# A decoder trunk with transposing DMAs: the transposes of a pass four blocks later in SP's order

## The chip, the cores and the metric

The kernel runs on one core of a Trainium2 chip. The metric is the device time in microseconds of one execution; several runs are taken and their median is used.

## The reference

Two decoder layers over one sequence of 256 tokens, width 2048, all in float32. The first mixes by pooling, the second by causal attention in blocks; both also attend to 256 memory tokens. Cut to what matters:

```python
for i in range(2):
    if i == 1:
        k_blocks, v_blocks, k_mean = moba_shared_kv(h, w_kv_shared)
    u = h @ w_in[i]                                   # (256, 2048) @ (2048, 4096)
    branch_in, gate_b, mem_q, gate_m = jnp.split(u, [1536, 3072, 3584], axis=-1)
    branch = multiscale_pool(branch_in, ...) if i == 0 else moba_attention(branch_in, ...)
    mem_o = memory_attention(mem_q, mem, w_mem_kv[i])  # 4 heads of 128
    mixed = concat([branch * silu(gate_b), mem_o * silu(gate_m)])
    h = layer_norm(4 ** 0.25 * h + mixed @ w_out[i], ln_g[i], ln_b[i])
```

`multiscale_pool` takes trailing means over 2, 4, 8 and 16 tokens in four groups of 384 columns, subtracts the token, and applies a 384 x 384 matrix per group and a scale. With 256 tokens and blocks of 256 the second layer's attention is plain causal softmax attention with 12 heads.

## The kernel before

**Blocks.** All weights are read once, in blocks of 128 x 1024 floats (512 KB; the pool matrices in pieces of 768 and 384 columns). The whole program is one list, `items`, of such blocks. `run()` walks over it; at step i it issues, in this order:

- `prep(i + 3)`: ACT writes the block's high part `wh`, VectorE the rest `wl = raw - wh` (`split`, L71 and L72). There are four `raw` buffers and four `wh`/`wl` pairs.
- `load(i + 4)`: the load into a `raw` buffer, on SP's queue (L99, L101). It waits until VectorE has split block i, which had that buffer.
- `consume` of block i: matmuls on TensorE, twelve with 512 columns for a whole block (high x high, high x low, low x high), into PSUM `acc`.
- the functions that were filed for step i with `later(n, fn)`, which means "n steps from now".

Each engine executes its instructions in the order in which they were issued, so this list is also the order on SP, ACT, VectorE and TensorE. An activation is split in the same way and stays in `xm` (the two halves `xT` and `memT`) or `zT`.

**Turned passes.** A pass (`proj_n`, eight blocks) gives 512 columns of a product with the tokens on the partitions, in two tiles t = 0, 1 of 128 tokens. Keys, queries, pool inputs and gates are needed with the columns on the partitions, and `turned` does that: ACT takes a float's two 16-bit halves apart ("planes", `pl`, L273), two transposing DMAs on SP's queue (L274) turn the planes of one t each, and later VectorE joins the halves (`join`, two copies, L284). There are 20 such passes, 8 of them for gates, in which ACT first forms a tanh (L268) and VectorE a product (L269) ahead of the planes. For keys and queries (`heads`) ACT then writes the high part (L291) in the step of the join and VectorE the low part (L292) one step later.

**Attention.** `plan(pr, a, turns, b, c)` files a pair of heads: at step `a` after the query pass the scores (matmuls into `s` from `kk` and `qq`), then exponentials (L330), division, 32 x 32 transposes on VectorE (`turns`, L354), splits of the probabilities `pp` (`b`), and the products with the values and the gating (`c`). The second layer does this in three groups of four heads: a group is a pass of keys (`w_sk`), of queries and of gates (`w_in`) and of values (`w_sv`, not turned; its split weights land in `memT`).

**Pool layer.** Three times a pass of four column tiles, then their gates; the small pool matrices are woven between the blocks of the following pass, and the gate tiles lie in a ring of seven slots.

Of the kernel before, what the change touches and what calls it, by code (L numbers as in the profile page):

```python
# [13 lines left out]
U16 = mybir.dt.uint16  # L14
AF = mybir.ActivationFunctionType
ALU = mybir.AluOpType
AX = mybir.AxisListType

P = 128
# [18 lines left out]
SLOTS = 7  # L38
# [2 lines left out]
LD0 = 8  # L41
IDLE = 9
LP = 3
JOIN = 3


@with_exitstack
def trunk(ctx: ExitStack, tc: tile.TileContext, a: dict, out: bass.AP):
    nc = tc.nc
    ctx.enter_context(tc.manual_schedule())  # L50
    sb = ctx.enter_context(tc.tile_pool(name="sb", bufs=1))
# [7 lines left out]
    xT, memT = kept = [xm[:, i * KX:(i + 1) * KX].rearrange("p (k t) -> p k t", k=KT) for i in range(2)]  # L59
# [6 lines left out]
    def mm(o, l, r, start, stop, **kw):  # L66
        nc.tensor.matmul(o, l, r, start=start, stop=stop, **kw)  # L67
# [17 lines left out]
    def item(src, cols, consume=None, dst=None):  # L85
        items.append(dict(src=src, cols=cols, consume=consume, dst=dst, cuts=(0, cols)))
# [5 lines left out]
    def later(n, fn):  # L92
        events[now[0] + n].append(fn)
# [102 lines left out]
    def cols(w, j):  # L196

        return [w[2 * j:2 * j + 2, b // 2, :, b % 2 * 512:(b % 2 + 1) * 512].rearrange("c p x -> p c x")
                for b in range(8)]

    def moving(w, src):

        if len(src.shape) == 3:
            return w.rearrange("p (c k n) -> p k c n", c=2, k=2)
        return w.rearrange("p (k n) -> p k n", n=512)

    def proj_n(sta, wblk, done, korder=range(8), banks=("acc", "acc"), place=None):

        acc = []
        korder = list(korder)  # L210

        def consume(j, kb):
            def go(wh, wl):
                if j == 0:
                    acc.extend(ps.tile([P, 512], F32, name=b, bufs=4 if b == "acc" else 1) for b in banks)
                h, l = (moving(w, wblk[kb]) for w in (wh, wl))
                for t in range(2):
                    for kk in range(2):
                        k = 2 * kb + kk
                        xh = sta[:, k, t * P:(t + 1) * P]  # L220
                        xl = sta[:, k, T + t * P:T + (t + 1) * P]
                        first, last = j == 0 and kk == 0, j == 7 and kk == 1
                        mm(acc[t], xh, h[:, kk], first, False)
                        mm(acc[t], xh, l[:, kk], False, False)
                        mm(acc[t], xl, h[:, kk], False, last)
                    if j == 7:
                        done(t, acc[t])
            return go
        for j, kb in enumerate(korder):
            item(wblk[kb], BLK, consume(j, kb), dst=place and ("keep", *place(j)))  # L230

    def pair():
        return sb.tile([P, 2 * T], F32, name="zf", bufs=2)
# [18 lines left out]
    in_res, in_q = home("res", 4 * D), home("qq", 4096)  # L252
# [5 lines left out]
    def turned(where, then, gate=False):  # L258

        tps, pls = [], []  # L260

        def done(t, acc):
            if not tps:
                tps.extend(where())
            src = acc
            if gate:
                src = pair()
                nc.scalar.activation(src, acc, AF.Tanh, scale=0.5)  # L268
                nc.vector.scalar_tensor_tensor(src, src, 1.0, acc, op0=ALU.add, op1=ALU.mult)  # L269
            if t == 0:  # L270
                pls.append(sb.tile([P, 2, 2, 512], U16, name="pl"))
            pl = pls[0][:, t]
            nc.scalar.activation(pl, src.bitcast(U16).rearrange("p (n h) -> p h n", h=2), AF.Copy)  # L273
            nc.sync.dma_start_transpose(tps[t], pl.rearrange("p h n -> p (h n)"))  # L274
            if t == 1:
                later(JOIN, lambda: then([tp.rearrange("p (h n) t -> p n h t", h=2) for tp in tps], pls[0]))
        return done

    def join(dst, tps, n0=0):
# [15 lines left out]
    def gates(slots, where):  # L295
        def then(tps, pl):
            n0 = 0
            while n0 < 4:
                n = 1
                while n0 + n < 4 and slots[n0 + n] == slots[n0] + n:  # L300
                    n += 1
                join(gate[:, slots[n0]:slots[n0] + n], tps, n0)
                n0 += n
        return turned(where, then, gate=True)
# [159 lines left out]
    def plan(pr, a, turns, b, c):  # L464

        later(a, pr.a)
        later(a + 1, pr.exps)
        later(a + 2, pr.divide)
        for g, t in enumerate(turns):
            later(t, lambda g=g: pr.turn(g))  # L470
        later(b, lambda: pr.b(0))
        later(b + 1, lambda: pr.b(1))
        later(c, pr.c)
# [93 lines left out]
    def after(fn):  # L567

        it = items[-1]
        old = it["consume"]  # L570

        def go(*w):
            if old is not None:
                old(*w)
            fn()
        it["consume"] = go

    def mem_q_gate(layer):
        q = fresh("q", lambda: heads_tile("qq"))
        where = in_ln if layer else in_res  # L580
        proj_n(xT, cols(a["w_in"][layer], 6), heads(q, where))
        prs = [MemPair(0, st), MemPair(2, st)]

        def go():
            plan(prs[0], 5, (8, 9, 10, 10), 11, 14)
            plan(prs[1], 12, (15, 17, 20, 22), 24, 27)
        after(go)
        proj_n(xT, cols(a["w_in"][layer], 7), gates(range(4), where))

# [19 lines left out]
    items.append(xs[2])  # L609
    rest = collect(mem_q_gate, 0)  # L610
    items += [rest[0], xs[3]] + rest[1:]
    after(lambda: later(JOIN + 1, pools))

    def pool_group(g):

# [35 lines left out]
    def pool_mix(g):  # L651
        zfs = []

        def consume(d0, nd):
            def go(wh, wl):
                h = wh[:, :3 * nd * P].rearrange("p (k n) -> p k n", k=3)
                l = wl[:, :3 * nd * P].rearrange("p (k n) -> p k n", k=3)
                for n in range(nd):
                    d = d0 + n
                    acc = ps.tile([P, 512], F32, name=("pt", "o", "s2")[d])[:, :T]  # L660
                    s = slice(n * P, (n + 1) * P)
                    for k in range(3):
                        kt = 3 * g + k
                        mm(acc, h[:, k, s], zT[:, kt, :T], k == 0, False)
                        mm(acc, h[:, k, s], zT[:, kt, T:], False, False)
                        mm(acc, l[:, k, s], zT[:, kt, :T], False, k == 2)
                    zf = zfs[0][:, T:] if d == 1 else pair()
                    zfs.append(zf)
                    zf = zf[:, :T]
                    nc.vector.scalar_tensor_tensor(zf, acc, psc[:, 3 * g + d:3 * g + d + 1],  # L670
                                                   gate[:, (3 * g + d) % SLOTS], op0=ALU.mult, op1=ALU.mult)
                if d0 + nd == 3:
                    zf = zfs[0].rearrange("p (j t) -> p j t", j=2)
                    split(zT[:, 3 * g:3 * g + 2, :T], zT[:, 3 * g:3 * g + 2, T:], zf)
                    split(zT[:, 3 * g + 2, :T], zT[:, 3 * g + 2, T:], zfs[2][:, :T])
            return go
        item(a["pool_a"][g], 768, consume(0, 2))
        item(a["pool_b"][g], 384, consume(2, 1))
# [24 lines left out]
    for c in range(3):  # L703
        weave(collect(proj_n, xT, cols(a["w_in"][0], c), to_pool(4 * c)), mixes, 5)
        items += mixes
        proj_n(xT, cols(a["w_in"][0], 3 + c), gates([(4 * c + d) % SLOTS for d in range(4)], in_q))
        mixes = sum((collect(pool_mix, g) for g in ((0,), (1,), (2, 3))[c]), [])
    after(lambda: later(3, load_x))

    weave(out_proj(0, range(4)), mixes, 5)  # L710

# [32 lines left out]
    for grp in range(3):  # L744
        k = fresh("k", lambda: heads_tile("kk"))
        q = fresh("q", lambda: heads_tile("qq"))
        v = fresh("v", val_tile)
        proj_n(xT, cols(a["w_sk"], grp), heads(k, in_ln))
        proj_n(xT, cols(a["w_in"][1], grp), heads(q, in_ln))
        prs = [MobaPair(2 * j, 4 * grp + 2 * j, st) for j in range(2)]  # L750

        def go(prs=prs, grp=grp):
            plan(prs[0], 5, (8, 9, 9, 10), 11, 18)
            plan(prs[1], 12, (15, 17, 18, 20), 22, 24)
        after(go)
        proj_n(xT, cols(a["w_in"][1], 3 + grp), gates(range(4), in_ln))
        proj_n(xT, [a["w_sv"][grp, kb] for kb in range(8)], to_values(v), place=in_mem)
# [101 lines left out]
    for _ in range(IDLE):  # L859
# [14 lines left out]
                                   op0=ALU.mult, op1=ALU.subtract)  # L874
# [72 lines left out]
```

## Time and profile before

| | |
|---|---|
| median of 3 runs | 882.15 us (878.69 to 882.46) |
| the profiled execution | 884.38 us, its span 882.6 us |
| matmul rows on TensorE | 3724, busy 826.9 us |
| VectorE busy, ACT busy | 603.7 us, 410.9 us |
| moved by DMA | 169.53 MB, mean 192 GB/s |
| mean granted clock of TensorE | 0.978 |

A busy share says how long an engine had an instruction under way, not what it did in that time. The waits say which instruction stood still and what let it go; the chain follows the last instruction back to the first. Times in a timeline run from the start of the span. Sequencers' rows (SPq) are the issuing of DMAs, not the transfers.

### The profile page before, as it was taken

The page shows a single profiled execution, that of the slowest core. Times are in us where ns is not written, and L with a number is a line of the kernel's source. Part 1 is how long each engine was busy: PE and PEld are TensorE (multiplying, and loading weights), DVE is VectorE, ACT ScalarE, POOL GpSimd, SP SyncE. Part 2 cuts the span into 40 slices and gives each one's busy share as a digit, 9 for nine tenths or more (in the row PEclk, how much of TensorE's full clock was granted, in tenths as well). Part 3 has the DMA queues.
Part 4 walks back from the last instruction along what each step waited for, and adds up shares of the span by engine and source line. Part 5 has one row for each costly group of instructions (what it writes and reads, how often), then busy time and mean ns, then how long its engine had stood idle before and what let it go on. Part 6 is the DMA issues. An engine that isn't in the chain of part 4 may idle for free.

```text
span 882.6 us, 10143 instructions
## 1 busy us (share of the span) xinstructions
PE 826.9 (94%) x3724; PEld 673.5 (76%) x3724; DVE 603.7 (68%) x839; ACT 410.9 (47%) x523; POOL 0.2 (0%) x4
## 2 busy tenths in 40 slices
PE   8999898999898999999989988999989997999997
PEld 6888676777776888888867766878777886878786
DVE  5674678657567775588446776786578854788946
ACT  6563544545344543445443454455445453545520
POOL 0000000000000000000000000000000000000000
PEclk9999999999999999999989999999989998999999
DMA  8876356555664866676655564547736567456852
GB/s 306 291 236 202 98 190 191 166 177 157 221 193 149 315 211 192 189 234 212 174 189 144 143 194 163 188 161 224 208 88 222 168 197 214 144 193 201 255 188 96
DMA packets 110021, 169.53 MB, mean 192 GB/s; under 512 B 47631, under 2 KB 49679, under 8 KB 109711
## 3 DMA queue, kind: packets, MB, share of 16 engines
q1 hardware_dynamic: 108656, 165.70, 60.6%
q10 hardware_dynamic: 1316, 3.19, 1.0%
q8 instruction: 29, 0.48, 0.3%
q14 instruction: 20, 0.16, 0.0%
HBM read 156.28 MB, written 2.10 MB: 179 GB/s over the span
## 4 chain that ended last, share of the span: by engine, by line
PE 44%; DVE 22%; DMA 15%; ACT 10%; issue 8%; SPq 1%; ACTq 0%; DVEq 0%
PE acc L67 38%; DMA raw<-in_w_in 10%; DVE wl L72 8%; ACT wh L71 5%; DVE p L354 3%; PE s L67 2%; ACT pl L273 2%; DMA raw<-in_w_out 2%; PE pt L67 1%; PE o L67 1%; DMA raw<-in_w_sv 1%; DVE xm L72 1%; ACT ebuf L330 1%; DVE zf L269 1%; DMA raw<-in_w_sk 1%
## 5 line engine op out<-in xcount | busy, mean ns | idle before, releaser
L67 PE MATMUL acc<-wh,xm 128*128 128x512 f32 x1344 | 429.1, 397 | 5.5 <-ACT wh L71 5.5
L72 DVE TENSOR_TENSOR wl<-raw,wh 128x1024 fp32r<-128x1024 f32 (+4 forms) x250 | 293.7, 1186 | 197.8 <-ACT wh L71 195.5
L71 ACT ACTIVATE wh<-raw 128x1024 fp32r<-128x1024 f32 (+4 forms) x250 | 251.8, 1025 | 223.4 <-DMA raw<-in_w_in 102.8
L67 PEld LDWEIGHTS acc<-wh,xm 128*128 128x128 f32 x1344 | 257.5, 192 | 61.2 <-ACT wh L71 8.1
L67 PE MATMUL acc<-wl,xm 128*128 128x512 f32 x672 | 268.5, 400 | 14.1 <-DVE wl L72 14.1
L67 PEld LDWEIGHTS acc<-wl,xm 128*128 128x128 f32 x672 | 128.7, 191 | 48.5 <-DVE wl L72 22.6
L67 PE MATMUL acc<-wh,zT 128*128 128x512 f32 x448 | 141.2, 393 | 2.3 <-ACT wh L71 2.3
L67 PEld LDWEIGHTS acc<-wh,zT 128*128 128x128 f32 x448 | 85.0, 190 | 20.7 <-ACT wh L71 3.2
L67 PE MATMUL acc<-wl,zT 128*128 128x512 f32 x224 | 88.8, 396 | 2.6 <-DVE wl L72 2.6
L67 PE MATMUL acc<-xm 128*128 128x512 f32 x288 | 67.5, 392 | 2.7 <-DVE xm L72 2.7
L67 PEld LDWEIGHTS acc<-xm 128*128 128x128 f32 x288 | 53.5, 188 | 15.3 <-DVE xm L72 4.5
L354 DVE STREAM_TRANSPOSE p<-ebuf 32x192 f32<-32x192 f32 (+1 forms) x160 | 63.3, 396 | 2.4
L72 DVE TENSOR_TENSOR xm<-raw,xm 128x1024 fp32r<-128x1024 f32 (+2 forms) x41 | 47.9, 1169 | 20.6 <-ACT xm L71 20.5
L71 ACT ACTIVATE xm<-raw 128x1024 fp32r<-128x1024 f32 (+2 forms) x41 | 41.1, 1009 | 27.6 <-DMA raw<-in_w_sv 16.0
L67 PEld LDWEIGHTS acc<-wl,zT 128*128 128x128 f32 x224 | 42.3, 189 | 13.9 <-DVE wl L72 5.3
L67 PE MATMUL s<-kk,qq 128*128 128x256 f32 (+1 forms) x108 | 20.7, 346 | 18.6 <-DVE qq L292 14.6
L67 PEld LDWEIGHTS s<-kk,qq 128*128 128x128 f32 x108 | 18.1, 243 | 22.1 <-DVE qq L292 15.6
L273 ACT ACTIVATE pl<-zf 128x1024 uint16<-128x1024 uint16 x16 | 16.9, 1058 | 18.8 <-DVE zf L269 18.8
L273 ACT ACTIVATE pl<-acc 128x1024 uint16<-128x1024 uint16 x24 | 23.9, 1015 | 3.9 <-PE acc L67 3.8
L67 PE MATMUL acc<-xm,wh 128*128 128x512 f32 x64 | 24.2, 420 | 1.1 <-ACT wh L71 1.1
L330 ACT ACTIVATE ebuf<-p,nb 128x128 f32<-128x128 f32 (+1 forms) x24 | 10.6, 445 | 29.5 <-DVE nb L326 29.5
L71 ACT ACTIVATE zT<-zf 128x512 fp32r<-128x512 f32 (+1 forms) x18 | 10.5, 581 | 27.4 <-DVE zf L360 22.2
(137 smaller groups left out, 530.6 us busy)
## 6 DMA issues: line engine op xcount, KB each, us to landing
raw<-in_w_in SPq DMA_DIRECT2D x128, 512.0 KB, 5.2
raw<-in_w_out SPq DMA_DIRECT2D x64, 512.0 KB, 4.5
raw<-in_w_sk SPq DMA_DIRECT2D x24, 512.0 KB, 4.2
raw<-in_w_sv SPq DMA_DIRECT2D x24, 512.0 KB, 3.5
raw<-in_w_mv SPq DMA_DIRECT2D x14, 512.0 KB, 5.6
raw<-in_w_mk SPq DMA_DIRECT2D x12, 512.0 KB, 4.9
raw<-in_xT SPq DMA_DIRECT2D x4, 512.0 KB, 4.4
res<-in_x ACTq DMA_DIRECT2D x2, 1024.0 KB, 6.5
```

The costliest lines, as they stand in the source:

```text
L67: nc.tensor.matmul(o, l, r, start=start, stop=stop, **kw)
L71: nc.scalar.activation(hi, src, AF.Copy)
L72: nc.vector.tensor_sub(lo, src, f(hi))
L269: nc.vector.scalar_tensor_tensor(src, src, 1.0, acc, op0=ALU.add, op1=ALU.mult)
L273: nc.scalar.activation(pl, src.bitcast(U16).rearrange("p (n h) -> p h n", h=2), AF.Copy)
L330: nc.scalar.activation(dst, src, AF.Exp, bias=self.nb[:, c:c + 1], scale=SCALE, accum_out=self.sm[:, c:c + 1])
L354: nc.vector.transpose(self.p[32 * g:32 * g + 32, h * self.n:(h + 1) * self.n], self.e[32 * h:32 * h + 32, g * self.n:(g + 1) * self.n])
```

## The change

Four things move; no instruction is added or taken away.

- The two transposes of a pass are filed four steps later (`SEND`), for gates five.
- The planes of a gate pass are filed one step later than its tanh and product.
- The join comes at step 4 instead of 3, for gates at step 6 (`JOIN + GATE`); the low part of keys and queries follows it, as before.
- All attention steps, the start of the pool buffers and the load of the residual come one step (pool buffers: three steps) later, and the slots of the pool layer's gates are counted from 4 instead of 0.

```diff
-JOIN = 3
+SEND = 4
+JOIN = 4
+GATE = 2
...
+        def planes(t, src):
+            nc.scalar.activation(pls[0][:, t], src.bitcast(U16).rearrange("p (n h) -> p h n", h=2), AF.Copy)
+
+        def send(t):
+            nc.sync.dma_start_transpose(tps[t], pls[0][:, t].rearrange("p h n -> p (h n)"))
+
         def done(t, acc):
...
-            pl = pls[0][:, t]
-            nc.scalar.activation(pl, src.bitcast(U16).rearrange("p (n h) -> p h n", h=2), AF.Copy)
-            nc.sync.dma_start_transpose(tps[t], pl.rearrange("p h n -> p (h n)"))
+                later(1, lambda: planes(t, src))
+            else:
+                planes(t, acc)
+            later(SEND + gate, lambda: send(t))
             if t == 1:
-                later(JOIN, lambda: then(...))
+                later(JOIN + GATE * gate, lambda: then(...))
...
-            plan(prs[0], 5, (8, 9, 10, 10), 11, 14)
+            plan(prs[0], 6, (9, 10, 11, 11), 12, 15)
...
-    after(lambda: later(JOIN + 1, pools))
+    after(lambda: later(JOIN + GATE + 1, pools))
...
-    after(lambda: later(3, load_x))
+    after(lambda: later(4, load_x))
...
-            plan(prs[0], 5, (8, 9, 9, 10), 11, 18)
+            plan(prs[0], 6, (9, 10, 10, 11), 12, 19)
```

SP's queue in the second group of heads, before (`w_sk` keys, `w_in` queries and gates, `w_sv` values; the weights in the first row are the group's keys and in the last the next group's):

```order
L99 DMA raw<-in_w_sk 128x2x512 x8
L99 DMA raw<-in_w_in 128x2x512 x4
L274 DMA_TRANSPOSE ln_g<-pl 128x8x128 x2
L99 DMA raw<-in_w_in 128x2x512 x8
L274 DMA_TRANSPOSE ln_g<-pl 128x8x128 x2
L99 DMA raw<-in_w_in 128x2x512 x4
L101 DMA raw<-in_w_sv 128x1024 x4
L274 DMA_TRANSPOSE ln_g<-pl 128x8x128 x2
```

The same place after the change:

```order
L101 DMA raw<-in_w_sk 128x2x512 x7
L101 DMA raw<-in_w_in 128x2x512 x8
L268 DMA_TRANSPOSE ln_g<-pl 128x8x128 x2
L101 DMA raw<-in_w_in 128x2x512 x8
L268 DMA_TRANSPOSE ln_g<-pl 128x8x128 x2
L103 DMA raw<-in_w_sv 128x1024 x8
L101 DMA raw<-in_w_sk 128x2x512
L268 DMA_TRANSPOSE ln_g<-pl 128x8x128 x2
```

The transposes of keys and queries stand behind all eight loads of the following pass instead of four, those of the gates behind nine.

ACT in the same group, before, from the planes of the queries (`pl<-acc`) to the planes of the gates (`pl<-zf`):

```order
L273 ACTIVATE pl<-acc 128x1024 x2
L71 ACTIVATE wh<-raw 128x1024 x3
L291 ACTIVATE qq<-pl 128x4x256
L71 ACTIVATE wh<-raw 128x1024 x2
L71 ACTIVATE xm<-raw 128x1024
L330 ACTIVATE ebuf,sm<-p,nb 128x4x32 x2
L330 ACTIVATE ebuf,sm<-p,nb 128x2x4x32 x2
L71 ACTIVATE xm<-raw 128x1024 x2
L268 ACTIVATE zf<-acc 128x512
L273 ACTIVATE pl<-zf 128x1024
```

And after:

```order
L265 ACTIVATE pl<-acc 128x1024 x2
L73 ACTIVATE wh<-raw 128x1024 x4
L298 ACTIVATE qq<-pl 128x4x256
L73 ACTIVATE wh<-raw 128x1024
L73 ACTIVATE xm<-raw 128x1024 x2
L337 ACTIVATE ebuf,sm<-p,nb 128x4x32 x2
L337 ACTIVATE ebuf,sm<-p,nb 128x2x4x32 x2
L73 ACTIVATE xm<-raw 128x1024
L276 ACTIVATE zf<-acc 128x512 x2
L73 ACTIVATE xm<-raw 128x1024
L265 ACTIVATE pl<-zf 128x1024 x2
```

The queries' high part stands behind the split of one more block, the exponentials too, and a split stands between a gate pass's two tanhs and its planes. (`xm<-raw` here is the split of a block of `w_sv`.)

More of the change, by code (lines that the diff above doesn't have):

```diff
@@ L260, in turned @@
         tps, pls = [], []
+        def planes(t, src):
+            nc.scalar.activation(pls[0][:, t], src.bitcast(U16).rearrange("p (n h) -> p h n", h=2), AF.Copy)
+        def send(t):
+            nc.sync.dma_start_transpose(tps[t], pls[0][:, t].rearrange("p h n -> p (h n)"))
         def done(t, acc):
-            if not tps:
+            if t == 0:
                 tps.extend(where())
-            src = acc
+                pls.append(sb.tile([P, 2, 2, 512], U16, name="pl"))
             if gate:
@@ L269, in done @@
                 nc.vector.scalar_tensor_tensor(src, src, 1.0, acc, op0=ALU.add, op1=ALU.mult)
-            if t == 0:
-                pls.append(sb.tile([P, 2, 2, 512], U16, name="pl"))
-            pl = pls[0][:, t]
-            nc.scalar.activation(pl, src.bitcast(U16).rearrange("p (n h) -> p h n", h=2), AF.Copy)
-            nc.sync.dma_start_transpose(tps[t], pl.rearrange("p h n -> p (h n)"))
+                later(1, lambda: planes(t, src))
+            else:
+                planes(t, acc)
+            later(SEND + gate, lambda: send(t))
             if t == 1:
-                later(JOIN, lambda: then([tp.rearrange("p (h n) t -> p n h t", h=2) for tp in tps], pls[0]))
+                later(JOIN + GATE * gate, lambda: then([tp.rearrange("p (h n) t -> p n h t", h=2) for tp in tps], pls[0]))
         return done
@@ L584, in go @@
         def go():
-            plan(prs[0], 5, (8, 9, 10, 10), 11, 14)
-            plan(prs[1], 12, (15, 17, 20, 22), 24, 27)
+            plan(prs[0], 6, (9, 10, 11, 11), 12, 15)
+            plan(prs[1], 13, (16, 18, 21, 23), 25, 28)
         after(go)
@@ L670, in go @@
                     nc.vector.scalar_tensor_tensor(zf, acc, psc[:, 3 * g + d:3 * g + d + 1],
-                                                   gate[:, (3 * g + d) % SLOTS], op0=ALU.mult, op1=ALU.mult)
+                                                   gate[:, (3 * g + d + 4) % SLOTS], op0=ALU.mult, op1=ALU.mult)
                 if d0 + nd == 3:
@@ L705, in trunk @@
         items += mixes
-        proj_n(xT, cols(a["w_in"][0], 3 + c), gates([(4 * c + d) % SLOTS for d in range(4)], in_q))
+        proj_n(xT, cols(a["w_in"][0], 3 + c), gates([(4 * c + d + 4) % SLOTS for d in range(4)], in_q))
         mixes = sum((collect(pool_mix, g) for g in ((0,), (1,), (2, 3))[c]), [])
-    after(lambda: later(3, load_x))
+    after(lambda: later(4, load_x))
     weave(out_proj(0, range(4)), mixes, 5)
@@ L752, in go @@
         def go(prs=prs, grp=grp):
-            plan(prs[0], 5, (8, 9, 9, 10), 11, 18)
-            plan(prs[1], 12, (15, 17, 18, 20), 22, 24)
+            plan(prs[0], 6, (9, 10, 10, 11), 12, 19)
+            plan(prs[1], 13, (16, 18, 19, 21), 23, 25)
         after(go)
```

## The prediction

> **What bounds the kernel now.** I read the page first, then who waits for whom on TensorE and on SP's queue, the granted clock, and last the rows around one pass.
>
> ```profile
> span 882.6 us, 10143 instructions
> PE 826.9 (94%) x3724; PEld 673.5 (76%) x3724; DVE 603.7 (68%) x839; ACT 410.9 (47%) x523; POOL 0.2 (0%) x4
> PE 44%; DVE 22%; DMA 15%; ACT 10%; issue 8%; SPq 1%; ACTq 0%; DVEq 0%
> ```
>
> TensorE is busy for 94% of the span, but only 44% of the chain that ended last is TensorE; 15% is DMA and 22% VectorE. So the end is set by a mixture, and it pays to price TensorE's pauses.
>
> ```profile
> PE acc L67 <- DVE wl L72: 16.7, 19, 1.9
> PE s L67 <- DVE qq L292: 14.6, 5, 3.0
> PE acc L67 <- ACT wh L71: 8.9, 8, 2.3
> PE s L67 <- ACT qq L291: 4.1, 5, 1.0
> PE acc L67 <- DVE xm L72: 2.7, 3, 1.3
> PE o L67 <- DVE pp L72: 1.3, 2, 1.0
> ```
>
> (Columns: total us, times, longest.) 28.3 us are waits for a block's split weights (16.7 + 8.9 + 2.7, 30 times), 18.7 us waits for the joined queries in five attention passes, 1.3 us for probabilities: 48.3 us in 42 pauses. Pauses also cost clock:
>
> ```profile
> 92.20:95.60 3.40, 2.98 (x12) 0.50 0.68 213
> 201.40:204.80 3.40, 3.40 (x10) 0.50 0.88 245
> 228.70:232.10 3.40, 3.40 (x10) 0.50 0.62 201
> 283.30:286.70 3.40, 3.40 (x10) 0.50 0.35 82
> 744.10:751.00 6.90, 5.56 (x18) 0.51 0.44 152
> sum 37.70, PE 33.70; mean PE 4.21
> 305.17 76.19 PE acc L67 x336
> ```
>
> The first rows are stretches of TensorE alone (length, busy time, matmuls, granted clock); the sum covers all eight stretches between start and end in which the clock stood at half, each behind a pause. Half of 37.7 is 18.8 us lost. The last row, from the chain, is a stretch without a turned pass: 76.19 / 336 = 0.227 us per matmul, so a block of 12 takes 2.72 us. A matmul row is 0.39 long, so a pause costs about 0.16 beyond its idle time: 42 x 0.16 = 6.7. All that pauses cost is 48.3 + 18.8 + 6.7 = 73.8 us.
>
> Where the pauses come from shows in the pass of the queries of group 2. Rows of SP, ACT, VectorE and TensorE in turn:
>
> ```profile
> 624.51 3.31 SPq L274 DMA_TRANSPOSE ln_g<-pl  x2
> 627.93 2.05 SPq L99 DMA_DIRECT2D raw<-in_w_in  x4
> 624.82 1.02 ACT L273 ACTIVATE pl<-acc 128x1024 uint16<-128x1024 uint16 x1 [0.34 <-PE acc L67]
> 625.74 1.05 ACT L71 ACTIVATE wh<-raw 128x1024 fp32r<-128x1024 f32 x1
> 633.31 1.06 ACT L71 ACTIVATE wh<-raw 128x1024 fp32r<-128x1024 f32 x1 [6.52 <-DMA raw<-in_w_in]
> 638.37 1.06 ACT L291 ACTIVATE qq<-pl 128x1024 fp32r<-128x1024 f32 x1 [2.65 <-DVE pl L284]
> 634.40 2.58 DVE L72 TENSOR_TENSOR wl<-raw,wh 128x1024 fp32r<-128x1024 f32 x2 [6.35 <-ACT wh L71]
> 636.90 1.38 DVE L284 COPY pl<-ln_g 128x1024 uint16<-128x1024 uint16 x2
> 640.41 1.23 DVE L72 TENSOR_TENSOR wl<-raw,wh 128x1024 fp32r<-128x1024 f32 x1 [2.13 <-ACT wh L71]
> 641.55 1.22 DVE L292 TENSOR_TENSOR qq<-pl,qq 128x1024 fp32r<-128x1024 f32 x1
> 639.48 0.39 PE L67 MATMUL s<-kk,qq 128*128 128x256 f32 x1 [1.00 <-ACT qq L291]
> 642.82 2.29 PE L67 MATMUL s<-kk,qq 128*128 128x128 f32 x9 [2.96 <-DVE qq L292]
> ```
>
> Call the pass's last block e and its end zero (624.8, where ACT's second plane starts). SP stands at the transposes until the planes are there, spends 1.25 us on issuing each, and reaches the load of block e+5 at +3.1. That load's buffer was free much earlier: block e+1 may be split once block e-3 has been consumed, at -8.2, and is done 1.06 + 1.23 later, at -5.9. So the load is 9.0 us late. ACT idles 6.5 us for it, VectorE 6.4 us, and behind that stand the join, the high part, the low part (done 642.8); TensorE loses 4.0 us there and goes to half clock. Ahead of that the buffered blocks carry TensorE. SP's own waits say the same of all twenty passes:
>
> ```profile
> SPq L274 <- ACT zf L268: 85.0, 8, 12.7
> SPq L274 <- ACT pl L273: 78.2, 12, 9.5
> ```
>
> These 163 us are what SP stands at transposes with loads queued behind (8 gate passes, 12 others).
>
> ```profile
> 546.20:574.00 27.80, 27.80 (x126) 22.42 (x125) 21.52 (x42) 12.88 (x21) 0.00 (x0) 1.00 0.48 151
> 585.00:624.00 39.00, 39.00 (x180) 32.34 (x179) 29.29 (x39) 20.58 (x24) 0.00 (x0) 1.00 0.64 198
> ```
>
> (Length, busy time of PE, PEld, DVE, ACT, POOL, clock, DMA share.) In the first stretch, attention steps run beside weights, in the second a pass of keys is turned, and TensorE never pauses: one late load is carried by the buffers (4 raw, 4 split), a late load followed by a deadline is not.
>
> **The change, part by part.** *Transposes later in SP's order.* Nothing is added or removed: 40 transposes of 1.25 us, 20 passes. With the new order SP meets them behind the load of e+8 (gates: e+9). That load needs block e+4 split: its split buffer comes free at 0, ACT first finishes the plane (+1.0), then 1.06 and 1.23: +3.3. Issued by +3.7; the transposes, whose planes are long done, occupy SP until +6.2. The next load, e+9, is due when e+5 is split, at 2.72 + 2.29 = +5.0; so it is 1.2 us late instead of 9.0.
>
> ```profile
> L274 SPq DMA_TRANSPOSE ln_g<-pl x22: 1232/1247/2297, 436.9 to 760.9; - x22
> DMA to landing us min/median/max: 3.0/3.2/5.0
> raw<-in_w_in SPq DMA_DIRECT2D x128, 512.0 KB, 5.2
> ```
>
> With the usual 5.2 us it lands at +11.4, and ACT can use it only once e+5 is consumed, at +13.6. That wait is gone for all passes: what I gain from it is nearly all the 28.3 us for split weights. It hides under 2.2 us of buffer; if that cover went, each further us would be one of ACT's, not at once TensorE's. What remains is the start, which has no turned pass ahead of it:
>
> ```profile
> 6.69 0.80 PE L67 MATMUL acc<-xm,wh 128*128 128x512 f32 x1 [1.06 <-ACT wh L71]
> ```
>
> *Joins one block later, two more for gates.* The join stands behind the split of e+7, which cannot end before 8.16 + 2.29 = +10.5. The second transpose, issued at +5.0, lands at +8.2, or +10.0 by the slowest landing seen. So VectorE doesn't wait. Both ends, since a transpose right behind a load in flight does not occur in this trace: nothing (landing 3.2), or, if the transpose first waits out the load ahead (issued at +3.3, landed 5.2 later at +8.5) and then takes its 3.2, +11.7 and 1.2 us of VectorE per pass, within the spare time worked out under the rivals. I take 0, since both orders issue into a queue that drains at the same rate. The Trainium skill, "DMA: Bandwidth & Descriptors", section "Queues, rings and completion order", says that each DMA engine takes descriptors in ring order, which speaks against this move; by it the value would be the upper end. No run so far shows it.
>
> *Attention steps one block later.* Join 10.5 to 11.9, high part to 13.0, ACT's split of e+8 to 14.0, VectorE's to 15.3, low part to 16.5; TensorE comes to the scores after block e+6, at 16.3, and to the first use of a low part 0.1 to 0.2 later. So about 0.2 us remain of what is 18.7 / 5 = 3.7 per attention pass, and I budget 0.3. With a join at e+3 and loads in time the old order would have had the same margin; the shift only keeps it. An attention step itself costs the same; the last pair of a group ends one block later, long before its columns are read.
>
> *Gates' planes one block later.*
>
> ```profile
> 554.70 3.53 SPq L274 DMA_TRANSPOSE ln_g<-pl  x2
> 553.61 1.06 ACT L273 ACTIVATE pl<-zf 128x1024 uint16<-128x1024 uint16 x1 [1.11 <-DVE zf L269]
> 562.92 1.06 ACT L71 ACTIVATE xm<-raw 128x1024 fp32r<-128x1024 f32 x1 [5.00 <-DMA raw<-in_w_sv]
> ```
>
> ACT no longer stands 1.1 us between tanh and plane while VectorE forms the product; two planes (2.1 us) come after the split of e+4 instead of before it. ACT has 53% idle, so neither sign reaches TensorE: 0. The gate slots are renumbered by four, which costs no instruction.
>
> *The sum.* 73.8 us can be had. I keep 1.1 (start), 5 x 0.3 = 1.5 (queries), 1.3 (probabilities), and, as an estimate for what the tighter schedule shows instead, 0.5 us in each of the 20 passes, 10, with 3 of the 6.7 for restarts. The half clock goes wholly, as the trace has it only behind the long pauses. Left: 16.9; gain 56.9. Since pool passes have smaller blocks, which the clean stretches above don't cover, I take 3 less: 53.9. The profiled execution took 884.4 us (span 882.6): 830.5. The median of the runs, 882.15, lies 2.2 lower: 828.
>
> On the clock the page "TensorE: Matmul & The Clock Gate" of the Trainium skill, Part 1, lets the clock fall to half after an idle window of about 3.4 us. The trace has stretches of that length at 0.50, but behind pauses of at most 3.0 us. By the page's wording alone no half clock would belong here at all; the measured stretches decide.
>
> **Rivals.** *The low part is still late.* Join and scores both move by one block, so the queries' margin stays as thin as in the order before. If VectorE is behind by 3 us for another reason, 18.7 us, 10 restarts (1.6) and the half clock of those passes stay (37.7 less the three stretches at 201, 229 and 283, 27.5 us, half 13.8): 34.1 less the 1.5 budgeted, 828 + 33 = 861. Against it: VectorE's lateness there is the 6.35 us wait quoted. Chance 0.12.
>
> *VectorE or ACT takes over in the pool and attention passes.* VectorE is busy 21.5 of 27.8 us in the first clean stretch. If half the waits for split weights stay (13) with the three pool stretches at half clock (5) and their restarts (2): 848. Chance 0.15.
>
> *Slower: transposes queue behind loads and the joins hold VectorE.* A join waiting at +10.5 delays the splits behind it. Spare: landing may come 5.5 us after the second issue for no wait; then the split of e+8, done at +15.3, may slip 3.7 us until TensorE needs it at 7 x 2.72 = 19.0; and to eat the gain it must cost a further 54 / 20 = 2.7 us per pass. So it decides from a landing 11.9 us after issue, against 3.2 median, 5.0 slowest, and 11.7 - 5.0 = 6.7 with a whole load ahead. At 14 us: 20 x 2.1 = 42 slower, 924. Chance 0.05.
>
> *No change:* the loads are late because four go out together and DMA is slow, not because of SP: 882. Against: they were issued 9.0 us late. Chance 0.04.
>
> **How the numbers follow.** The forecast has 0.64; its own range is 813 (all but start, queries and probabilities regained, 73.8 - 3.9, so 812.3) to 843 (0.5 us more per pass, 10, and a quarter of the half clock, 5). With the second rival and the near side of the first the range is 813 to 853, which leaves out some 0.2. A measurement tells 0.5%, some 4.4 us, from no change: faster 0.91, same 0.03, slower 0.06.
>
> **What would show it.** Right: SP's waits at transposes drop from 163 us to a few; ACT's longest wait for weights is under 3 us; waits of TensorE for queries total under 3 us; no half clock after the start. Wrong: transposes landing beyond 7 us, VectorE waiting at the joins, or the half-clock stretches standing where they were.

## The result and the profile after

The changed kernel takes 811.73 us (809.1 to 814.85, 4 runs) against 880.82 us (878.69 to 882.46, 4 runs): a ratio of 0.9218, 95% interval 0.9175 to 0.9262. The forecast was 828 us with 813 to 853: the direction and the cause held, the size was too small, and the time lies 1.3 us below the range. The profiled execution took 813.1 us, its span 811.1.

Three lines of the page after the change:

```profile
span 811.1 us, 10158 instructions
PE 798.5 (98%) x3724; PEld 664.2 (82%) x3724; DVE 604.5 (75%) x841; ACT 411.0 (51%) x523; POOL 0.2 (0%) x4
PE 86%; DVE 7%; issue 2%; DMA 2%; ACT 2%; SPq 0%; DVEq 0%; ACTq 0%
```

The chain that ended last is now 86% TensorE (44% before), and DMA has fallen from 15% of it to 2%. VectorE and ACT are busy for as long as before. TensorE's idle time went from 882.6 - 826.9 = 55.7 to 12.6 us, and its busy time fell by 28.4 us for the same 3724 matmuls.

Who TensorE waits for after the change (total us, times, longest), without the start's first memset and the last two lines of under 0.5 us:

```profile
PE s L69 <- DVE qq L299: 2.4, 1, 2.4
PE acc L69 <- DVE wl L74: 2.3, 4, 1.0
PE acc L69 <- ACT wh L73: 0.8, 1, 0.8
```

The 48.3 us in 42 pauses have become 5.5 us in 6. Of the eight stretches at half clock one is left between start and end, behind the 2.4 us pause:

```profile
494.90:498.30 3.40, 3.40 (x10) 2.71 (x9) 3.03 (x7) 0.46 (x3) 0.00 (x0) 0.50 0.60 211
```

SP's longest waits:

```profile
SPq L101 <- DVE wl L74: 278.7, 121, 5.8
SPq L103 <- DVE wl L74: 159.1, 79, 6.7
SPq L103 <- DVE xm L74: 57.3, 26, 3.7
```

No line for the transposes (L268) is among SP's waits any more: the 163 us are gone, and SP now waits for buffers, as a queue that runs ahead should. How late the loads come shows in ACT, which splits them. Its waits for blocks of `w_in`, before and after:

```profile
ACT wh L71 <- DMA raw<-in_w_in: 102.8, 50, 6.9
ACT wh L73 <- DMA raw<-in_w_in: 15.8, 13, 3.3
```

The queries' pass of group 2, which the prediction worked through, on ACT, SP and VectorE after the change:

```profile
571.08 1.02 ACT L265 ACTIVATE pl<-acc 128x1024 uint16<-128x1024 uint16 x1 [0.29 <-PE acc L69]
582.95 1.06 ACT L298 ACTIVATE qq<-pl 128x1024 fp32r<-128x1024 f32 x1 [2.65 <-DVE pl L291]
574.76 4.05 SPq L268 DMA_TRANSPOSE ln_g<-pl  x2
578.91 20.39 SPq L103 DMA_DIRECT2D raw<-in_w_sv  x8
580.34 1.23 DVE L74 TENSOR_TENSOR wl<-raw,wh 128x1024 fp32r<-128x1024 f32 x1 [1.49 <-ACT wh L73]
581.48 1.38 DVE L291 COPY pl<-ln_g 128x1024 uint16<-128x1024 uint16 x2
584.99 1.23 DVE L74 TENSOR_TENSOR wl<-raw,wh 128x1024 fp32r<-128x1024 f32 x1 [2.13 <-ACT wh L73]
586.14 1.22 DVE L299 TENSOR_TENSOR qq<-pl,qq 128x1024 fp32r<-128x1024 f32 x1
```

With zero at 571.1, the transposes are issued at +3.7 (forecast +3.7), the join starts at +10.4 (+10.5), the high part at +11.9 (+11.9), the low part ends at +16.3 (+16.5). TensorE has no pause there. One thing is off: the two transposes hold SP for 4.05 us instead of 2.5, so the next load leaves at +7.8 instead of +6.2; the buffers cover it in this pass.

### The profile page after: what moved, and what is told of

Its sections match the earlier page's. It is cut to its first block, busy times and chain, and to the rows that moved or that the text cites. A ratio compares the mean times of both kernels' runs of the same rounds, so it can differ in the third digit from the quotient of the medians.

```text
span 811.1 us, 10158 instructions
## 1 busy us (share of the span) xinstructions
PE 798.5 (98%) x3724; PEld 664.2 (82%) x3724; DVE 604.5 (75%) x841; ACT 411.0 (51%) x523; POOL 0.2 (0%) x4
## 4 chain that ended last, share of the span: by engine, by line
PE 86%; DVE 7%; issue 2%; DMA 2%; ACT 2%; SPq 0%; DVEq 0%; ACTq 0%
PE acc L69 79%; PE s L69 3%; DVE wl L74 2%; PE o L69 2%; PE pt L69 2%; DVE p L361 1%; DMA raw<-in_w_in 1%; ACT wh L73 1%; DMA raw<-in_w_mk 1%; DVE xm L74 0%; DMA ln_g<-pl 0%; ACT ebuf L337 0%; DMA raw<-in_w_out 0%; SPq L268 0%; DVE res L488 0%
## 5 line engine op out<-in xcount | busy, mean ns | idle before, releaser
L69 PE MATMUL acc<-wh,xm 128*128 128x512 f32 x1344 | 421.4, 391 | 0.0
L69 PEld LDWEIGHTS acc<-wh,xm 128*128 128x128 f32 x1344 | 253.1, 188 | 52.3
L69 PE MATMUL acc<-wl,xm 128*128 128x512 f32 x672 | 262.6, 391 | 1.0 <-DVE wl L74 1.0
L69 PEld LDWEIGHTS acc<-wl,xm 128*128 128x128 f32 x672 | 126.7, 188 | 27.1 <-DVE wl L74 1.8
L69 PE MATMUL acc<-wh,zT 128*128 128x512 f32 x448 | 139.4, 390 | 0.0
L69 PE MATMUL acc<-xm,zT 128*128 128x256 f32 (+1 forms) x144 | 22.6, 318 | 0.0
L73 ACT ACTIVATE pp<-p 128x384 fp32r<-128x384 f32 (+1 forms) x20 | 11.2, 559 | 22.1 <-DVE p L361 22.1
L69 PEld LDWEIGHTS acc<-xm,zT 128*128 128x128 f32 x144 | 20.7, 190 | 1.9
L73 ACT ACTIVATE zT<-zf 128x512 fp32r<-128x512 f32 (+1 forms) x18 | 10.5, 581 | 22.2 <-DVE zf L367 17.5
```

What stands on the lines that cost most here:

```text
L73: nc.scalar.activation(hi, src, AF.Copy)
```

## The experiments

My theory was that the gain comes from SP's order: loads no longer stand behind transposes that wait for planes. The rival was that the later joins and attention steps give VectorE its time. Each run below is timed against the kernel before on the same chip.

**The later steps without the later transposes.** In the kernel after:

```diff
-                later(1, lambda: planes(t, src))
+                planes(t, src)
...
-            later(SEND + gate, lambda: send(t))
+            send(t)
```

> The kernel after, but transposes and gate planes where they were before (step 0 of a pass); joins and attention steps keep their later places. My theory (SP's queue: loads stand behind transposes that wait for planes) expects nearly the time of before, 870 to 890 us, SP standing some 160 us at transposes, TensorE waiting some 28 us for split weights and over 10 us for queries. The rival (the steps one block later are what gives VectorE the time) expects 812 to 825 us.

876.35 us, ratio 0.9946 (0.9926 to 0.9966). SP stands at the transposes as long as before:

```profile
SPq L268 <- ACT zf L276: 87.4, 8, 12.1
SPq L268 <- ACT pl L265: 80.6, 12, 9.8
```

TensorE's wait for the queries in the same run:

```profile
PE s L69 <- DVE qq L299: 12.5, 5, 2.8
```

The later steps alone give 5 us of the 69. The rival falls.

**One kind of pass at a time.** The 12 passes without gates late, the gate passes at once (`later(0 if gate else SEND, ...)`, the gates' planes at once):

> Only the 12 passes without gates send late (step 4); the 8 gate passes send at once, with their planes at once. In the trace of before the pauses that follow a pass without gates within some 20 us, their half clock included, come to about 45 us, those that follow a gate pass to about 24. My theory: 881 - 45 = 836 us (828 to 846). Rival (the gate passes matter most, since SP stood longer there, 85 us in 8 passes): 850 to 870 us.

And the other way round (`later(SEND + 1 if gate else 0, ...)`, the gates' planes one step later):

> Only the 8 gate passes send late (step 5, planes one step later); the 12 others send at once. My theory: 881 - 24 = 857 us (848 to 866), and this gain and that of the run with the others alone add up to about the whole 69 us. Rival (the passes disturb each other, so either alone gives little or nearly all): a sum of the two gains that is off from 69 us by more than 15.

849.9 us (0.9654, 0.9612 to 0.9697) and 834.66 us (0.9467, 0.9411 to 0.9524): 31 and 46 us. The two add up to 78 us against 69, so they overlap by 9 us only, but both times lie outside what I expected. My split by "what pauses within 20 us behind a pass" was wrong: I gave 45 us to the passes without gates and 24 to the gates. TensorE's waits say what each mends. With the passes without gates late:

```profile
PE acc L69 <- ACT wh L73: 9.3, 6, 2.2
PE acc L69 <- DVE wl L74: 8.2, 16, 1.2
PE s L69 <- DVE qq L299: 2.4, 1, 2.4
```

With the gates late:

```profile
PE s L69 <- DVE qq L299: 13.2, 5, 2.9
PE acc L69 <- DVE wl L74: 7.0, 10, 1.4
```

The queries are mended by the late transposes of their own pass (2.4 us left), the waits for ACT's high parts of weights (8.9 us before) by the late gates. Late gates also contain the deferred planes, which a later run prices at 12.5 us; without them, by an estimate, some 34 us would be left to the order of the gates' transposes, about as much as to that of the other passes.

**How far back is far enough.** `SEND = 1`:

> The kernel after with the transposes filed one step after the pass instead of four (gates: two instead of five). My theory in its arithmetic: SP then stands at them until the planes are there (+1.0 us) and reaches the next load at about +3.6, 6.9 us late instead of 9.0; TensorE is carried by the buffers, but the low part of the queries comes about 2 us late in five passes, with half clock: 825 to 840 us. Rival (it is enough that one more load stands ahead, the buffers do the rest): 811 to 818 us. Rival (all four blocks are needed): over 855 us.

822.01 us (0.9333, 0.9286 to 0.9381). That is 3 us below my figure and above the first rival's: with the transposes only one block back, the whole change still gives 59 of its 69 us, although SP still stands at the transposes. (The deferred planes, which a later run prices at 12.5 us, are among the 59.)

```profile
SPq L268 <- ACT pl L265: 89.7, 19, 6.7
```

TensorE's largest wait is then

```profile
PE s L69 <- DVE qq L299: 7.3, 5, 3.0
```

What is left is mostly the queries' low part, in five passes, as the arithmetic had it. `SEND = 3`:

> The kernel after with the transposes filed three steps after the pass (gates: four) instead of four (five). By my arithmetic they are then issued at about +1.0 to +3.5 us, just ahead of the load of e+8, which is due at +3.3: the load is not late, and the transposes land some 2.5 us earlier, so the one pass in which the join waited for its transpose and TensorE 2.4 us for the queries' low part (with 3.4 us of half clock) should be gone: 806 to 811 us. Rival (SP stands at the planes again): over 814 us.

809.92 us (0.9182, 0.9160 to 0.9204), within the expected figures, and not told apart from four blocks (0.9218, 0.9175 to 0.9262). SP does stand at the transposes again, in pauses that are too short to cost anything that shows:

```profile
SPq L268 <- ACT wh L73: 37.1, 24, 3.3
```

But the reason that I gave is only half right: the half clock went, the 2.4 us pause stayed. I had also run two passes together: the join that waits 2.1 us for its transpose is that of the keys, at 464 us, and not that of the queries ahead of the pause. VectorE's rows ahead of the pause, in the kernel after:

```profile
485.84 0.68 DVE L367 SCALAR_TENSOR_TENSOR zf<-o,gate 128x512 f32<-128x512 f32 x1
487.22 0.69 DVE L74 TENSOR_TENSOR zT<-zf,zT 128x512 fp32r<-128x512 f32 x1 [0.70 <-ACT zT L73]
487.83 1.40 DVE L291 COPY pl<-ln_g 128x1024 uint16<-128x1024 uint16 x2
492.50 1.22 DVE L299 TENSOR_TENSOR qq<-pl,qq 128x1024 fp32r<-128x1024 f32 x1
```

The second memory pair's gated product falls into the step of the queries' join (step 28 of its plan is step 4 of the next query pass) and stands ahead of it. With that step one block earlier (`25, 28` to `24, 27` in the memory pair's plan, on top of `SEND = 3`):

> The kernel with transposes at step 3, and the last two steps of the second memory pair one step earlier (24 and 27 instead of 25 and 28), so that its gated product no longer stands in the step of the next queries' join. If that collision is the cause of the one pause left (TensorE 2.4 us for the queries' low part at 492 us of the span), the pause goes: 806 to 808.5 us. Rival (the pause has another cause): 809 to 811 us, with the pause still there.

809.24 us (0.9173, 0.9146 to 0.9201), and the pause is halved:

```profile
491.59 1.33 PE L69 MATMUL s<-kk,qq 128*128 128x128 f32 x9 [1.14 <-DVE qq L299]
```

The time lies on the rival's side (809 to 811 us), as the pause is still there. By this one trace the collision is part of its cause, not all of it; what the other 1.1 us wait for stays open. This is the fastest version by its median, but its interval overlaps that of `SEND = 3`.

**The gates' planes.** The kernel after with `planes(t, src)` at once instead of one step later:

> The kernel after with the planes of a gate pass taken at once, as before, instead of one step later. My theory: ACT stands some 1 us per tile for VectorE's product, which nobody waits for: 811 to 816 us. Rival (ACT's stand delays the split of the next block, and this part carries some of the gain): 820 us or more.

824.28 us (0.9346, 0.9321 to 0.9372): 12.5 us more than after, or 11 by the ratios, as the two ran on different chips. My theory, and the price of zero in the prediction, were wrong, the rival right. In this run ACT waits for VectorE's product ahead of each of the 16 planes; in the kernel after it does so once, for 1.2 us:

```profile
ACT pl L265 <- DVE zf L277: 19.7, 16, 3.6
```

ACT and TensorE at the first gates of the pool layer:

```profile
145.95 0.57 ACT L276 ACTIVATE zf<-acc 128x512 f32<-128x512 f32 x1
150.12 1.06 ACT L265 ACTIVATE pl<-zf 128x1024 uint16<-128x1024 uint16 x1 [3.60 <-DVE zf L277]
152.42 1.06 ACT L265 ACTIVATE pl<-zf 128x1024 uint16<-128x1024 uint16 x1 [0.76 <-DVE zf L277]
154.48 0.50 PE L69 MATMUL acc<-wh,xm 128*128 128x512 f32 x1 [1.80 <-ACT wh L73]
155.74 0.80 PE L69 MATMUL acc<-wl,xm 128*128 128x512 f32 x1 [0.76 <-DVE wl L74]
```

VectorE is behind with pool and attention work, ACT stands 3.6 us for its product, the next block's high part comes late, and VectorE, which needs that, is idle in turn. TensorE loses 1.8 + 0.8 us, and behind that its clock stands at half for 6.8 us (from 154.9). In the kernel after ACT has two other instructions between tanh and plane:

```profile
145.37 1.06 ACT L276 ACTIVATE zf<-acc 128x512 f32<-128x512 f32 x2
146.32 1.05 ACT L73 ACTIVATE wh<-raw 128x1024 fp32r<-128x1024 f32 x1
147.69 0.64 ACT L73 ACTIVATE pp<-p 128x512 fp32r<-128x512 f32 x1 [0.31 <-DVE p L361]
149.54 2.01 ACT L265 ACTIVATE pl<-zf 128x1024 uint16<-128x1024 uint16 x2 [1.22 <-DVE zf L277]
```

**How much room VectorE has.** In the kernel after, `split` of a weight block is followed by

```diff
+        nc.vector.tensor_sub(wl[:, c0:c0 + 256], raw[:, :256], f(wh[:, c0:c0 + 256]))
```

> The kernel after, in which VectorE writes the first 256 columns of each block's low part a second time: some 0.35 to 0.43 us more in each of about 245 blocks, 90 to 100 us of VectorE in all, so it is busy for some 86% instead of 75%. It measures the room that the forecast set aside 0.5 us per pass for. If the room is wide (what the result suggests): 811 to 818 us. If the schedule is tight, as the forecast had it: the attention and pool passes pause again, 825 us or more.

855.83 us (0.9707, 0.9680 to 0.9733): the room is not wide. The largest group of the added instruction (busy us, mean ns, idle before):

```profile
L122 DVE TENSOR_TENSOR wl<-raw,wh 128x256 fp32r<-128x256 f32 x250 | 106.3, 425 | 8.6
```

TensorE's wait for low parts, 2.3 us in the kernel after, is

```profile
PE acc L69 <- DVE wl L122: 24.5, 22, 2.3
```

With the blocks whose low part lands in `xm`, and three more, the instruction stands 285 times, and VectorE's busy time is 720.9 instead of 604.5 us. These 116 us beside work that leaves VectorE idle for a quarter of the time cost 44 us: its 75% is an average over stretches with less room. Part of the 44 us may be plain delay, as each of these low parts is also ready 0.4 us later; the run does not part the two.

**The transposes on another queue.** The kernel before, with one word changed:

```diff
-            nc.sync.dma_start_transpose(tps[t], ...)
+            nc.scalar.dma_start_transpose(tps[t], ...)
```

> The kernel before, with nothing moved but the 40 transposes to ACT's queue: they are issued right behind the planes, at the old steps, and no load stands behind them; ACT spends 1.25 us more on each. My theory (the loads behind the transposes on SP were the whole cost): 812 to 832 us with joins and attention at the old steps. Rival (the later steps are needed too, or the early transposes disturb the loads): 845 us or more.

859.19 us (0.9739, 0.9705 to 0.9774), a miss, on the rival's side. SP stands at no transpose here, but ACT pays. Its idle time that no other engine or transfer ended, in the three groups where it is largest:

```profile
ACT wh L71 <- issue: 24.0, 14, 3.7
ACT pl L273 <- issue: 16.3, 11, 2.3
ACT zf L268 <- issue: 8.2, 6, 1.4
```

Not all of it is issuing: ahead of `wh` it is 2.8 us in the kernel before, but 14.0 in the kernel after, where ACT issues no transpose. But at the queries of group 2 the second transpose holds ACT for 3.54 us (from 605.7), and the next split stands 3.67 us for it. ACT feeds VectorE and so TensorE, and it is held right at the end of a pass, where the next split is due. So the run moves the standing from SP to ACT, and does not tell whether the later steps are needed. The next one does.

**One line.** The kernel before with the transposes filed two steps later and nothing else:

```diff
-            nc.sync.dma_start_transpose(tps[t], pl.rearrange("p h n -> p (h n)"))
+            later(2, lambda: nc.sync.dma_start_transpose(tps[t], pl.rearrange("p h n -> p (h n)")))
```

> The kernel before with one line changed: the transposes of all passes are filed two steps later, still ahead of the joins at step 3; joins, attention steps and the gates' planes stay as before. If the order on SP is the main cause and the gates' planes are worth some 12 us on top (as the run with the planes taken at once showed), this gives 824 us and a little for joins that now come just behind their transposes: 824 to 840 us. Rival (the later joins and attention steps are needed for the gain, as the run with the transposes on ACT's queue could be read): 850 us or more.

822.17 us (0.9319, 0.9289 to 0.9349), with joins, attention and planes as before. The order on SP is the main cause, by itself worth 60 us of the 69. The waits in this run, of SP at the transposes, of ACT for blocks of `w_in` and of TensorE for the queries:

```profile
SPq L274 <- ACT zf L268: 31.2, 8, 4.2
SPq L274 <- ACT wh L71: 27.1, 17, 4.5
SPq L274 <- ACT pl L273: 22.8, 9, 3.8
ACT wh L71 <- DMA raw<-in_w_in: 17.3, 17, 3.1
PE s L67 <- DVE qq L292: 2.5, 1, 2.5
```

SP still stands at transposes for 81 us by these lines, but never longer than 4.5 us at a time (12.7 before), and ACT's waits for loads are nearly as short as after the whole change. So what costs is not the total of SP's standing, but a hold that is longer than the blocks in the buffers last. The run with the planes at once has transposes four blocks back and joins and attention steps late, and takes 824.28 us; its interval overlaps that of this run. The later steps thus add nothing that these runs can tell, and what the whole change gives beyond the 60 us is, as far as they tell, the planes.

## Why the prediction was wrong in size and right in its main mechanism

**SP's order: right.** The pauses disappear as worked out, SP's waits at transposes are gone, and the pass that was followed step by step matches to 0.2 us, but for the issuing of the transposes. The one-line run shows that this order is enough for most of the gain. Of the four signs of being right, two came as stated (SP's waits at transposes, 2.4 us for the queries) and two were missed narrowly: ACT's longest wait for weights is 3.3 us instead of under 3, and one stretch of half clock is left.

**Joins and attention steps: right as "no gain by themselves".** With the transposes early they give 0.5%, and with the transposes two blocks back the old steps do as well. The rival "the low part is still late" came true in one of five passes, with 2.4 us, not in five with 3 us.

**The gates' planes: wrong; this is the step that failed.** It read "neither sign reaches TensorE: 0", with ACT's 53% idle time as the cover. That is an average; where VectorE is behind, ACT stands up to 3.6 us for the product, the next split comes late, and TensorE waits. The deferral is worth 12.5 us (824.28 against 811.73).

**The sum: the reserve was mis-sized.** Of 73.8 us I kept 19.9 (1.1 start, 1.5 queries, 1.3 probabilities, 10 for the passes, 3 restarts, 3 for the pool passes). Measured by the same tally, after the change there remain 5.5 us of waits, 6 x 0.16 = 1.0 for restarts and 3.4 / 2 = 1.7 of clock: 8.2. So 11.7 us too many were kept, most of them in the 10 us for the passes, of which 2.3 came. That is close to what the planes are worth: with the planes at once the time is 824.28 us, 4 from the forecast, and the same tally of that run gives 11.0 us of waits in 14 pauses, 2.2 of restarts and (6.8 + 3.4) / 2 = 5.1 of clock, 18.3 in all. So the reserve stood, in its total, for pauses that a part of the change, priced at nothing, removes. The items do not match (no half clock was reserved, 5.1 us came), so that the totals lie so near is partly luck.

**The tally was short, too.** The profiled execution fell by 884.4 - 813.1 = 71.3 us, of which the tally explains 73.8 - 8.2 = 65.6. It even counts 2.0 us twice: in the 37.7 us at half clock TensorE is busy for 33.7 only, and the other 4.0 are already among the waits, so that the clock cost 33.7 / 2 = 16.9 us and not 18.8. Without them 7.7 us are unexplained. The page shows where they are: TensorE's busy time fell by 28.4 us, of which 16.9 - 1.7 = 15.2 are clock and 6.7 - 1.0 = 5.7 restarts; some 7.5 us are neither. I take them for waits of under 0.16 us, which a row of 0.39 us hides at a spacing of 0.227, so that they count as busy; no run singled them out, and the cause of this part stays open. With the reserve alone right, 830.5 - 11.7 = 818.8 would have come out; the last 5.7 us to 813.1 are what the tally missed on balance.

**The rivals.** "VectorE or ACT takes over" did not happen here, but the room is not wide: 116 us more on VectorE cost 44. "Transposes queue behind loads" is there in kind and too small: landing went up to 6.4 us at most, as the next section but one shows, where 11.9 would have been needed, and VectorE waited at joins for 3.6 us in all.

## What to carry to other kernels

A DMA that waits for a computation, on a queue that also prefetches, holds every load behind it; file it where its data has long been ready, and count for each queue what stands behind the waiting instruction. Here it was enough that the hold became shorter than the buffers last: two blocks later, in one line, gave 60 of the 69 us. The same holds for an engine that waits for another in the middle of a chain: put other work between the two halves, and price such a wait at the busiest place, not by the engine's average. Ahead of a sum, ask whether "left over" costs are already paid by another part of the same change.

## What the runs showed of the hardware

Where the transposes are issued right behind loads, they held their queue longer and landed later. The rows of the kernel after (ns, shortest, median, longest; then us to landing):

```profile
L268 SPq DMA_TRANSPOSE ln_g<-pl x22: 1231/1794/4227, 406.1 to 695.4; - x22
DMA to landing us min/median/max: 3.2/4.7/6.4
```

Before, where SP had stood for the planes while the loads ahead were landing, issuing took a median of 1.25 us and at most 2.3 in that group, and the landing a median of 3.2 and at most 5.0. With `SEND = 1`, where SP stands at most transposes too, the medians are again 1.25 and 3.2. Ring order, as the Trainium skill has it in "DMA: Bandwidth & Descriptors", "Queues, rings and completion order", agrees with the later landing (6.4 at most, 6.7 estimated with a load ahead); the longer hold of the issuing queue I had not expected. But ring order is not singled out: with the transposes on ACT's queue, where the loads of the weights do not stand ahead of them, landing took as long (a median of 4.9 us, at most 9.4), and issuing, with a median of 1.25 us, up to 3.5. So loads in flight on the other queue may be enough.

The clock fell to half for 3.4 us behind a pause of 2.4 us in the kernel after, while a pause of the same 2.4 us with `SEND = 3` left it at full (1.00 from 491.9 to 495.3 us): whether such a pause costs clock is not settled by its length alone.
